# A transformer layer on one core: SP's loads and VectorE's operations in source order, the conditioning row spread by TensorE, exponentials queued behind the last sigmoid

## The chip, the core and the metric

The kernel runs on one core of a Trainium2 chip. Its time is the device time in microseconds of one execution. A core has five engines with a queue each: TensorE (PE in the profile, its weight loads PEld), VectorE (DVE), ScalarE (ACT), GpSimd (POOL) and SyncE (SP), which here only issues DMAs. Each engine does its queue in order, and engines wait for each other by semaphores.

## What is computed

One layer over 1024 latent tokens of 1024 channels, with 256 context tokens. In short:

```python
mod = silu(c) @ w_mod + b_mod                       # six vectors of 1024
h   = x * (1 + scale1) + shift1
h_c = ctx * (1 + scale_c) + shift_c                 # from silu(c_ctx) @ w_mod[:, :2048]
proj = h @ w_in + b_in                              # q_a, k_a, v_a, q_b, k_b, v_b, gate logits
q_a, k_a = rope(...); q_b, k_b = rope(rms_norm(...))
o_a = windowed attention(+-128 tokens, sink) over latent and context keys
o_b = global attention over latent and context keys
y = (sigmoid(g_a) * (o_a @ w_a) + sigmoid(g_b) * (o_b @ w_b)) @ w_out
x = layer_norm(alpha * x + gate1 * y)
x = layer_norm(alpha * x + gate2 * conv_ffn(x * (1 + scale2) + shift2))
```

All is float32. The large products are made of three float32r matmuls: each operand is split into a high part (a cast) and a low part (the difference), and high x high, high x low and low x high are added (`split`, line 79; `mm3`, line 88).

## The kernel before

**First projection (lines 222 to 238).** `h` stands transposed, eight blocks of 128 channels by 1024 tokens. `spread` (line 175) loads c into all 128 partitions by a broadcast DMA and applies Silu, which gives `sc`. For each block k, `load1` fetches two rows of w_mod (`wm`), a block of the weight of q_b (`wr`) and one of x. `modulate` splits the weight (ACT casts the high part, VectorE makes the low part `wlqb`), reduces each `wm` with `sc` on VectorE to a column of `modc` (`mod`, line 186: one multiply-and-add reduction over 128x1024), and makes the high and low parts `hh`, `hl` of h (ACT, ACT, VectorE). Then 24 matmuls add the block to the eight accumulators `q1acc`. `scc`, the same from c_ctx, follows.

**The remaining projections (lines 691 to 738).** `order` is a list of steps: 16 gates (`g`, 48 matmuls each, two halves of 24) are dealt out between the groups qa, qb (8 steps of 12 matmuls each), ka, kb (8 steps of 15: keys and values, four halves of the context among the tiles of kb): 3 gates, qa, 4 gates, qb, 4 gates, ka, 1 gate, kb, 4 gates. `prefetch` (line 616) loads and splits the weights of coming steps; raw weights rotate over 3 buffers and split ones over 8, four pairs. `mods` (line 643) spreads 48 more reductions (`wml` rows of w_mod, 512 KB each) evenly over the steps up to the end of ka: when one is due, it issues its load and its reduction. `gate` ends with a Sigmoid on ACT and a store of the result. `side_step` runs waiting pieces after each step: `qpost` (sums of squares and rotation of queries), `kv_post` (the same for keys, and the splits and transposes `ktr` that fill KL and KC), `qprep` of the first attention units. Accumulators are evacuated at the end of a group by VectorE (`q_evac`; `kv` in line 728).

**What sets the order.** The source gives the dependences; the order on each engine is made by a scheduler with a model of the machine, so an operation can move far from its place in the source. Buffers are reused in rotation: an operation that writes a tile waits for the last use of its buffer. Large temporaries share 19 slots (`ht`, `hput`, lines 129 to 138).

**Passage to the attention (lines 739 to 743).** So that ACT's exponentials, which need another function table than Sigmoid, come behind the last Sigmoid, a tiny chain stands there: VectorE makes zeros out of the last gate's result, ACT takes their Exp, and VectorE adds the zeros to `sinkb`. Then come the attention units (`Unit`, line 383): scores on TensorE, the minimum on VectorE (line 458), Exp on ACT (`soft`, line 424), transposes, values, and the rest of the layer, which the change doesn't touch.

Of the kernel before, what the change touches and what calls it, by code (L numbers as in the profile page):

```python
# [60 lines left out]
VSPAN = 1.0  # L61
VSC = 0, 1
DNS = {u0 + 2 * n + (u0 == 20): (n, j0, j1) for u0, j0, j1 in ((16, 0, 4), (20, 4, 8), (24, 8, 11)) for n in range(3)}


@with_exitstack
def layer_kernel(
# [33 lines left out]
    bmc = ctile([P, 48], F32, "bmc")  # L101
    nc.scalar.dma_start(bmc, bmod)
    modx = ctile([P, 16], F32, "modx")
# [10 lines left out]
    onesf = ctile([P, P], F32, "onesf")  # L114
    mhalf = ctile([P, 8], F32, "mhalf")
    nc.vector.memset(onec, 1.0)
# [89 lines left out]
    def modulate(k):  # L206
        wm, x, wr = st1.pop(k)
        w = wsplit(wr, f"qb{k}")
        for j in (0, 1):
            col = j * 8 + k  # L210
            mod(wm[j], sc, bmc[:, col:col + 1], modc[:, col:col + 1])
        hh = hTp.tile([P, T], R32, tag="hT", name=f"hh{k}", bufs=16)
        hl = hTp.tile([P, T], R32, tag="hT", name=f"hl{k}", bufs=16)
        a, b = modc[:, k:k + 1], modc[:, 8 + k:9 + k]
        for s in [slice(0, HALF), slice(HALF, T)] if k == 0 else [slice(0, T)]:
            nc.scalar.activation(hh[:, s], x[:, s], AF.Identity, bias=a, scale=b)
# [62 lines left out]

    def rms_scale(x3, H, nm, sq, ss=None):  # L280
        nc.scalar.activation(sq.rearrange("p (h d) -> p h d", d=HD), x3, AF.Square)
        if ss is None:
            ss = ph1.tile([P, 8], F32, tag="ss", name=f"ss{nm}", bufs=4)[:, 0:H]
# [21 lines left out]
    def qpost(br, t):  # L305
        q = qtile(br, t)
        q3 = q.rearrange("p (h d) -> p h d", d=HD)
        if br == 0:
            def r0():
                rope(nc.gpsimd if t % 3 == 2 else nc.vector, q, q, 8, ropec[:, t], ropes[:, t], f"q0_{t}")  # L310
            return [r0]
        st = {}

        def s1():
            st["tb"] = ph1.tile([P, 2, HD], F32, tag="tb", name=f"tbq{t}", bufs=4)
            gfold(st["tb"], 0, t, nc.gpsimd)
            rms_scale(q3, 8, f"q{t}", sqq[0][:, t % 2], pqs[:, t])
            if t == NT - 1:
                sqq.clear()
                hput("sqq")  # L320
            nc.gpsimd.tensor_scalar(out=nqs[:, t], in0=pqs[:, t], scalar1=-1.0, scalar2=0.0, op0=ALU.mult, op1=ALU.add)
# [6 lines left out]
    sqq = [ht("sqq", (P, 2, 512))]  # L328
    bias_qb = bias_tile(b_qb, "bias_qb")
    for t in range(NT):  # L330
        q_evac(1, t, acc[t], bias_qb)

    KL, KC, VT = [], [], []
# [7 lines left out]

    def kv_post(t, kv):
        st = {}
        kb = kv[:, 128:256].rearrange("p (h d) -> p h d", d=HD)

        def s1():
            vt = VT[t // 2][:, t % 2]
            v3 = kv[:, 256:512].rearrange("p (h d) -> p h d", d=HD)
# [9 lines left out]

        def s2():
            rms_apply(kb, 2, st["ss"])  # L360
            tp = st["tp"]
# [21 lines left out]
    class Unit:  # L383
# [40 lines left out]
        def soft(self, s, p, h, nm, sm, scale):  # L424
            nc.scalar.activation(p, s, AF.Exp, bias=nm[:, h:h + 1], scale=scale, accum_out=sm[:, h:h + 1])  # L425

# [188 lines left out]

    def prefetch(gi, k):
        if gi == "g":
            hs = []
            for a in (0, 1):
                wr = raw(f"wg{k}_{a}")  # L620
                nc.sync.dma_start(wr.rearrange("p (a b) -> p a b", b=P), w_g[k][:, 4 * a:4 * a + 4])
                hs.append(wsplit(wr, f"g{k}_{a}", "gpsimd"))
            ready[gi, k] = hs
            return
        nm, src, tiles = groups[gi]
        wr = raw(f"w{nm}{k}")
        nc.sync.dma_start(wr, src[k])
        c = None
        if NT in tiles:
            cx = ph1.tile([P, NC], F32, tag="cx", name=f"cx{k}", bufs=2)  # L630
            nc.sync.dma_start(cx, ctxT[k])
            nc.scalar.activation(cx, cx, AF.Identity, bias=modx[:, k:k + 1], scale=modx[:, 8 + k:9 + k])
            c = [ph1.tile([P, NC], R32, tag="ch", name=f"c{a}{k}", bufs=4) for a in "hl"]
            split(cx, *c, nc.vector, nc.vector)
        ready[gi, k] = wsplit(wr, f"{nm}{k}"), c

# [3 lines left out]
    total = len(late)  # L640
    span = [0.0, 0.0]

    def mods(us):
        span[0] += us
        n = total - len(late)
        for _ in range(min(int(total * span[0] / span[1] + 0.01) - n, len(late))):
            col, row, o = late.pop(0)
            w = tmp(f"wml{len(late)}")
            nc.sync.dma_start(w, wmodT[col])
            mod(w, row, bmc[:, col:col + 1], o)  # L650
            if not late:
                hput("sc", "scc")
                kv_alloc()

    def gate(f, hf):
        ps = acc_tile(f"g{f}_{hf}")
        s = slice(hf * HALF, (hf + 1) * HALF)
        for k in range(KT):
            h, l = ready["g", f][k // 4]
            n = slice(k % 4 * P, (k % 4 + 1) * P)  # L660
            mm3(ps, (h[:, n], l[:, n]), (hT[k][0][:, s], hT[k][1][:, s]), k == 0, k == KT - 1)
        if late:
# [4 lines left out]
        nc.scalar.activation(sg, ps, AF.Sigmoid, bias=bgc[:, f:f + 1])  # L667
        nc.scalar.dma_start(sgd[f][:, s], sg)
        return sg

# [25 lines left out]
    ahead = [2 if gi in (0, 2, 3) else 4 for gi, _ in order]  # L696
    span[1] = sum(6 * KT if gi == "g" else 3 * len(groups[gi][2])
                  for gi, _ in order[:order.index((0, KT - 1)) + 1])
    nxt = 0
    for n, (gi, k) in enumerate(order):  # L700
        while nxt < len(order) and sum(ahead[n:nxt + 1]) <= 8:
            prefetch(*order[nxt])
            nxt += 1
        if gi == "g":
            for hf in (0, 1):
                last = gate(k, hf)
                mods(3 * KT)
# [6 lines left out]
        w, c = ready.pop((gi, k))  # L714
        for t in tiles:
            if t < NT:
                s = slice(t * P, (t + 1) * P)
                a = hT[k][0][:, s], hT[k][1][:, s]
            else:
                s = slice((t - NT) * P, (t - NT + 1) * P)  # L720
                a = c[0][:, s], c[1][:, s]
            mm3(acc[t], a, w, k == 0, k == KT - 1)
        mods(3 * len(tiles))
        if k == KT - 1:
            for t in tiles:
                if gi < 2:
                    kv = ph1.tile([P, 512], F32, tag="kv", name=f"kv{t}", bufs=KVB)
                    nc.vector.tensor_tensor(out=kv, in0=acc[t], in1=bias_kv, op=ALU.add)
                    queue.append(kv_post(t, kv))
                else:  # L730
# [11 lines left out]
    nc.scalar.activation(zero, zero, AF.Exp)  # L742
    nc.vector.tensor_tensor(out=sinkb[:, 0:4], in0=sinkb[:, 0:4], in1=zero, op=ALU.add)
    hTp.release()
# [1005 lines left out]
```

## Time and profile before

| | |
|---|---|
| median of 3 runs | 1578.19 us (1576.92 to 1581.11) |
| the profiled execution | 1580.51 us |
| its span in the profile | 1578.6 us, granted clock 0.994 |
| busy PE, DVE, ACT, POOL | 97%, 76%, 51%, 48% of the span |
| first projection q1 starts | 12.87 us |
| first gate starts | 59.06 us |
| attention's first scores | 344.79 us |

The profile is one execution as the hardware profiler took it. A line of a timeline has the start in us, the duration, the engine, the line of the source, the operation, the tile written and those read, the shape, and in brackets how long the engine was idle before and what ended that. A matmul's duration overlaps the next one's; the distance of two starts is the pace. The view of waits has an engine and line, what it waited for, the sum in us, the count and the longest.

### The profile page before, as it was taken

Reading aid. Unit: us, or ns where it says so; the run is one execution under the profiler, and the core shown is the slowest. Engines: PE = TensorE matmul, PEld = TensorE weight load, DVE = VectorE, ACT = ScalarE, POOL = GpSimd, SP = SyncE. Lnnn points to the kernel's source line nnn. Section 1 sums busy time; section 2 is a strip of 40 time slices with the busy share of each in tenths; the row PEclk is TensorE's granted clock in tenths of the full one; section 3 lists DMA queues with packets and bytes.
Section 4 is the critical chain, followed back from the end, with each engine's and each line's share of the span. In section 5 each row is a group of like instructions: output and inputs, shape, how many; then the busy total and the mean of one; then the engine's idle time right before and its main releaser. Section 6 shows DMA issues by size and latency. Waiting matters only on the chain.

```text
span 1578.6 us, 21930 instructions
## 1 busy us (share of the span) xinstructions
PE 1528.4 (97%) x7614; PEld 1264.6 (80%) x7614; DVE 1198.0 (76%) x1761; ACT 808.9 (51%) x1439; POOL 756.5 (48%) x737
## 2 busy tenths in 40 slices
PE   6999999999999999999999999999999999999997
PEld 5878788878886887777788898888888888888886
DVE  7797645628888777788675679888888888656797
ACT  5422222448888667688522466444444444435533
POOL 0573312426666566655432544666667765021053
PEclk9999999999999999999999999999999999999999
DMA  9685662322227555532344132333334446996723
GB/s 378 218 313 187 213 219 87 120 79 74 64 82 180 138 128 127 128 84 41 130 160 93 54 107 81 121 107 107 107 107 107 107 111 178 364 270 221 244 92 107
DMA packets 112015, 230.25 MB, mean 146 GB/s; under 512 B 13504, under 2 KB 27328, under 8 KB 111808
## 3 DMA queue, kind: packets, MB, share of 16 engines
q1 hardware_dynamic: 96464, 199.20, 37.9%
q0 software_dynamic: 10400, 20.19, 8.2%
q10 hardware_dynamic: 5040, 9.46, 1.6%
q8 instruction: 60, 0.98, 0.3%
q14 instruction: 51, 0.42, 0.1%
HBM read 177.61 MB, written 65.87 MB: 154 GB/s over the span
## 4 chain that ended last, share of the span: by engine, by line
PE 73%; DVE 12%; DMA 5%; ACT 4%; issue 3%; POOL 1%; SPq 0%; ACTq 0%; DVEq 0%; POOLq 0%
PE ptr L530 5%; PE b L91 3%; PE b L90 3%; PE b L89 3%; PE g L89 3%; PE g L91 3%; PE g L90 3%; PE s L413 2%; PE av L551 2%; PE c L90 2%; PE d L90 2%; PE a L90 2%; PE c L89 2%; PE d L89 2%; PE a L89 2%
## 5 line engine op out<-in xcount | busy, mean ns | idle before, releaser
L540 DVE TENSOR_TENSOR ptl<-ptr,pth 128x512 fp32r<-128x512 f32 x188 | 124.6, 684 | 27.8 <-ACT pth L539 25.6
L86 DVE TENSOR_TENSOR ld<-rd,hd 128x1024 fp32r<-128x1024 f32 x77 | 97.6, 1284 | 50.8 <-ACT hd L81 48.7
L530 PE MATMUL ptr<-ident,p 128*128 128x128 f32 x816 | 126.7, 278 | 9.2 <-DVE ptl L540 6.8
L539 ACT CAST pth<-ptr 128x512 fp32r<-128x512 f32 x188 | 106.5, 588 | 56.5 <-PE ptr L530 32.8
L425 ACT ACTIVATE p<-p,nm 128x1024 f32<-128x1024 f32 (+2 forms) x128 | 125.3, 981 | 11.1 <-DVE p L458 10.3
L530 PEld LDWEIGHTS ptr<-ident,p 128*128 128x128 f32 x816 | 93.6, 140 | 39.6 <-DVE ptl L540 13.9
L81 ACT CAST hd<-rd 128x1024 fp32r<-128x1024 f32 x77 | 79.4, 1050 | 88.5 <-PE p L91 60.4
L551 PE MATMUL av<-pth,VT 128*128 128x512 f32 x236 | 104.6, 443 | 1.0 <-ACT avs L557 0.5
L90 PE MATMUL p<-ld,hd 128*128 128x512 f32 x264 | 103.5, 392 | 0.3 <-DVE ld L86 0.3
L89 PE MATMUL p<-hd 128*128 128x512 f32 x264 | 103.8, 393 | 0.0
L91 PE MATMUL p<-hd,ld 128*128 128x512 f32 x264 | 103.5, 392 | 0.0
L89 PE MATMUL g<-hh,whg 128*128 128x512 f32 x256 | 99.9, 390 | 0.0
L91 PE MATMUL g<-hh,wlg 128*128 128x512 f32 x256 | 99.7, 389 | 0.0
L90 PE MATMUL g<-hl,whg 128*128 128x512 f32 x256 | 99.6, 389 | 0.0
L552 PE MATMUL av<-ptl,VT 128*128 128x512 f32 x236 | 97.7, 414 | 1.9 <-POOL ptl L86 1.8
L86 POOL TENSOR_TENSOR wlg<-wg,whg 128x512 fp32r<-128x512 f32 x32 | 44.2, 1388 | 112.7 <-ACT whg L81 109.2
L458 DVE TENSOR_SCALAR_CACHE_REDUCE p<-s,cvt,nmc 128x1024 f32<-128x1024 f32 x64 | 84.4, 1339 | 12.3 <-PE s L414 11.8
L413 PE MATMUL s<-KL,q 128*128 128x512 f32 (+2 forms) x192 | 76.0, 396 | 2.9 <-ACT p_x L425 2.0
L187 DVE CUSTOM_DVE_ANT_0 wml<-wml,sc,bmc 128x1024 f32<-128x1024 f32 x32 | 45.6, 1435 | 40.6 <-DMA wml<-in_wmodT_dram 39.7
L83 POOL TENSOR_SCALAR pth<-prw 128x512 fp32r<-128x512 f32 x48 | 31.0, 646 | 87.8 <-ACT prw L536 62.3
L414 PE MATMUL s<-KL,q 128*128 128x512 f32 (+2 forms) x192 | 71.7, 373 | 0.0
L81 ACT CAST wS<-s 128x512 fp32r<-128x512 f32 x76 | 45.3, 621 | 51.0 <-POOL s L1083 50.2
(402 smaller groups left out, 4945.7 us busy)
## 6 DMA issues: line engine op xcount, KB each, us to landing
wml<-in_wmodT_dram SPq DMA_DIRECT2D x48, 512.0 KB
ru<-in_w_up_dram SPq DMA_DIRECT2D x38, 512.0 KB
rd<-td SPq DMA_DIRECT2D x55, 256.0 KB
rd<-sd SPq DMA_DIRECT2D x44, 256.0 KB
rd<-in_w_dn_dram SPq DMA_DIRECT2D x33, 256.0 KB
wm<-in_wmodT_dram SPq DMA_DIRECT2D x16, 512.0 KB
wg<-in_w_g_dram SPq DMA_DIRECT2D x32, 256.0 KB
sgd<-sg ACTq DMA_DIRECT2D x32, 256.0 KB
```

Of the source, the lines that this page charges most:

```text
L81: cast[:] = [nc.scalar.copy(hi, src).ins]
L86: low[:] = [lo_eng.tensor_tensor(out=lo, in0=src, in1=hi.bitcast(F32), op=ALU.subtract).ins]
L89: nc.tensor.matmul(ps, a[0], b[0], start=start, stop=False, skip_group_check=resumed)
L90: nc.tensor.matmul(ps, a[0], b[1], start=False, stop=False, skip_group_check=resumed)
L91: nc.tensor.matmul(ps, a[1], b[0], start=False, stop=stop, skip_group_check=resumed)
L413: nc.tensor.matmul(o, self.q[0][:, hs], ks, start=True, stop=False)
L425: nc.scalar.activation(p, s, AF.Exp, bias=nm[:, h:h + 1], scale=scale, accum_out=sm[:, h:h + 1])
L530: nc.tensor.transpose(tr[:, h * P:(h + 1) * P], self.pslice(h, n), ident)
L539: nc.scalar.copy(hi, tr)
L540: nc.vector.tensor_tensor(out=lo, in0=tr, in1=hi.bitcast(F32), op=ALU.subtract)
L551: nc.tensor.matmul(self.av, v, hi, start=first, stop=False)
L552: nc.tensor.matmul(self.av, v, lo, start=False, stop=self.left == 0)
```

## The change

- c is loaded as one row of 4 KB. TensorE spreads it over the partitions: two float32 matmuls with a row of ones; Silu reads the halves from PSUM. Five matmuls of ones by ones stand ahead of them and twelve behind, whose results nobody uses. In block 0 the weight's split comes behind the two reductions.
- The sums of squares of q_b are made for two tiles at a time, ahead of their rotation: four instructions of double width on ACT, VectorE and GpSimd in place of eight.
- `prefetch` is taken apart: loads (`wload1`) run 5 steps ahead of the matmuls, splits (`wpair`) 3; a gate counts as two steps. The loads of `wml` (`mload`) run 4 ahead of the reductions. From there to the end of ka, SP and VectorE keep the source's order (`manual_schedule`); the other engines, and the rest of the kernel, are left to the scheduler.
- The evacuation of keys and values moves from the group's end into the first piece of `kv_post`.
- The chain of zeros goes. One Exp of 8 columns with nothing to compute is issued behind the last Sigmoid, and each `soft` behind it.

```diff
+WARM = 5, 12
+WLOAD = 5
+WSPLIT = 3
+MLOAD = 4
...
-    nc.scalar.dma_start(bmc, bmod)
...
+    crow = hp.tile([1, D], F32, tag="H18", name="crow", bufs=1)
+    nc.scalar.dma_start(crow, c_row.rearrange("(a d) -> a d", a=1))
+    nc.scalar.dma_start(bmc, bmod)
...
     def modulate(k):
         wm, x, wr = st1.pop(k)
-        w = wsplit(wr, f"qb{k}")
+        if k:
+            w = wsplit(wr, f"qb{k}")
         for j in (0, 1):
             col = j * 8 + k
             mod(wm[j], sc, bmc[:, col:col + 1], modc[:, col:col + 1])
+        if k == 0:
+            w = wsplit(wr, f"qb{k}")
...
-    spread(sc, c_row, 0)
+    cb = [acc_tile(f"cb{n}") for n in (0, 1)]
+    for n in range(WARM[0]):
+        nc.tensor.matmul(cb[1][:, 0:P], onesf, onesf, start=True, stop=True)
+    for n in (0, 1):
+        s = slice(n * HALF, (n + 1) * HALF)
+        nc.tensor.matmul(cb[n], onesf[0:1], crow[:, s], start=True, stop=True)
+        nc.scalar.activation(sc[:, s], cb[n], AF.Silu)
+    wt_ = acc_tile("warm")
+    for n in range(WARM[1]):
+        nc.tensor.matmul(wt_[:, 0:P], onesf, onesf, start=True, stop=True)
...
         def s1():
             st["tb"] = ph1.tile([P, 2, HD], F32, tag="tb", name=f"tbq{t}", bufs=4)
             gfold(st["tb"], 0, t, nc.gpsimd)
-            rms_scale(q3, 8, f"q{t}", sqq[0][:, t % 2], pqs[:, t])
...
+            if t % 2 == 0:
+                qstats(t)
...
+    def qsquare(t):
+        nc.scalar.activation(sqq[t // 2 % 2].rearrange("p a b -> p (a b)"), Q[1, t].rearrange("p a b -> p (a b)"),
+                             AF.Square)
+
+    def qstats(t):
+        sq = sqq[t // 2 % 2]
+        ss, ns = (a[:, t:t + 2].rearrange("p a b -> p (a b)") for a in (pqs, nqs))
+        nc.vector.tensor_reduce(out=ss, in_=sq.rearrange("p a (h d) -> p (a h) d", d=HD), axis=AX.X, op=ALU.add)
+        if t + 4 < NT:
+            qsquare(t + 4)
+        nc.vector.tensor_scalar(out=ss, in0=ss, scalar1=1.0 / HD, scalar2=QK_EPS, op0=ALU.mult, op1=ALU.add)
+        nc.gpsimd.tensor_tensor(out=ss, in0=ss, in1=mhalf[:, 0:16], op=ALU.pow)
+        nc.gpsimd.tensor_scalar(out=ns, in0=ss, scalar1=-1.0, scalar2=0.0, op0=ALU.mult, op1=ALU.add)
...
         def s1():
+            kv = st["kv"] = ph1.tile([P, 512], F32, tag="kv", name=f"kv{t}", bufs=KVB)
+            nc.vector.tensor_tensor(out=kv, in0=acc, in1=bias_kv, op=ALU.add)
...
         def soft(self, s, p, h, nm, sm, scale):
-            nc.scalar.activation(p, s, AF.Exp, bias=nm[:, h:h + 1], scale=scale, accum_out=sm[:, h:h + 1])
+            with tc.issue_after(first_exp):
+                nc.scalar.activation(p, s, AF.Exp, bias=nm[:, h:h + 1], scale=scale, accum_out=sm[:, h:h + 1])
...
+    def mload():
+        col, row, o = late.pop(0)
+        w = tmp(f"wml{len(late)}")
+        nc.sync.dma_start(w, wmodT[col])
+        coming.append((col, row, o, w))
...
-            col, row, o = late.pop(0)
-            w = tmp(f"wml{len(late)}")
-            nc.sync.dma_start(w, wmodT[col])
+            col, row, o, w = coming.pop(0)
             mod(w, row, bmc[:, col:col + 1], o)
-            if not late:
+            if late:
+                mload()
+            elif not coming:
...
+    held = steps.index((0, KT - 1, 0)) + 1
+    inorder = ExitStack()
+    inorder.enter_context(tc.manual_schedule(engines={mybir.EngineType.DVE, mybir.EngineType.SP}))
+    for n in range(WLOAD):
+        at(n, wload1)
+        if n + WSPLIT - WLOAD >= 0:
+            at(n + WSPLIT - WLOAD, wpair)
+    for _ in range(MLOAD):
+        mload()
+    for n, (gi, k, a) in enumerate(steps):
+        if n == held:
+            inorder.close()
+        at(n + WLOAD, wload1)
+        at(n + WSPLIT, wpair)
+        at(n + 3, cload, 1)
+        at(n + 2, cpair, 1)
...
-    zero = ph1.tile([P, 4], F32, tag="zero", name="zero")
-    nc.vector.tensor_scalar(out=zero, in0=last[:, 0:4], scalar1=-(2.0 ** 100), scalar2=None, op0=ALU.min)
-    nc.scalar.activation(zero, zero, AF.Exp)
-    nc.vector.tensor_tensor(out=sinkb[:, 0:4], in0=sinkb[:, 0:4], in1=zero, op=ALU.add)
+    with tc.issue_after(sigmoid[0]):
+        first_exp = nc.scalar.activation(lnx[:, 0:8], negsink, AF.Exp).ins
```

More of the change, by code (lines that the diff above doesn't have):

```diff
@@ L114, in layer_kernel @@
     onesf = ctile([P, P], F32, "onesf")
[L115 removed]
+    mhalf = ctile([P, 24], F32, "mhalf")
     nc.vector.memset(onec, 1.0)
@@ L278, in gfold, with rms_scale @@
             eng.tensor_tensor(out=dv[:, :, a, :], in0=sv[:, :, a, :], in1=gv[:, :, 1 - a, :], op=ALU.mult)
-    def rms_scale(x3, H, nm, sq, ss=None):
+    def rms_scale(x3, H, nm, sq):
         nc.scalar.activation(sq.rearrange("p (h d) -> p h d", d=HD), x3, AF.Square)
-        if ss is None:
-            ss = ph1.tile([P, 8], F32, tag="ss", name=f"ss{nm}", bufs=4)[:, 0:H]
+        ss = ph1.tile([P, 8], F32, tag="ss", name=f"ss{nm}", bufs=4)[:, 0:H]
         nc.vector.tensor_reduce(out=ss, in_=sq.rearrange("p (h d) -> p h d", d=HD), axis=AX.X, op=ALU.add)
@@ L326, in qpost @@
         return [s1] + [lambda: None] * GAP + [s2]
-    sqq = [ht("sqq", (P, 2, 512))]
+    sqq = [ht(f"sqq{n}", (P, 2, 512)) for n in (0, 1)]
+    def qsquare(t):
[10 more added lines that the diff above has]
+        nc.gpsimd.tensor_scalar(out=ns, in0=ss, scalar1=-1.0, scalar2=0.0, op0=ALU.mult, op1=ALU.add)
+        if t + 2 == NT:
+            hput("sqq0", "sqq1")
     bias_qb = bias_tile(b_qb, "bias_qb")
@@ L331, in layer_kernel @@
         q_evac(1, t, acc[t], bias_qb)
+        if t in (1, 3):
+            qsquare(t - 1)
     KL, KC, VT = [], [], []
@@ L340, in layer_kernel, with kv_post @@
     bias_kv = bias_tile(b_kv, "bias_kv")
-    def kv_post(t, kv):
+    def kv_post(t, acc):
         st = {}
-        kb = kv[:, 128:256].rearrange("p (h d) -> p h d", d=HD)
         def s1():
+            kv = st["kv"] = ph1.tile([P, 512], F32, tag="kv", name=f"kv{t}", bufs=KVB)
+            nc.vector.tensor_tensor(out=kv, in0=acc, in1=bias_kv, op=ALU.add)
+            kb = st["kb"] = kv[:, 128:256].rearrange("p (h d) -> p h d", d=HD)
             vt = VT[t // 2][:, t % 2]
@@ L359, in s2 @@
         def s2():
+            kv, kb = st["kv"], st["kb"]
             rms_apply(kb, 2, st["ss"])
@@ L614, in layer_kernel, with wload1, wpair, cload @@
     ready = {}
-    def prefetch(gi, k):
+    def wload1(gi, k, a):
         if gi == "g":
[L618 to L635, printed above, removed]
+            wr = raw(f"wg{k}_{a}")
+            nc.sync.dma_start(wr.rearrange("p (a b) -> p a b", b=P), w_g[k][:, 4 * a:4 * a + 4])
+        else:
+            wr = raw(f"w{groups[gi][0]}{k}")
+            nc.sync.dma_start(wr, groups[gi][1][k])
+        ready[gi, k, a, "raw"] = wr
+    def wpair(gi, k, a):
+        wr = ready.pop((gi, k, a, "raw"))
+        if gi == "g":
+            ready[gi, k, a] = wsplit(wr, f"g{k}_{a}", "gpsimd")
+        else:
+            ready[gi, k, a] = wsplit(wr, f"{groups[gi][0]}{k}")
+    def cload(gi, k):
+        cx = ready["cx", k] = ph1.tile([P, NC], F32, tag="cx", name=f"cx{k}", bufs=2)
+        nc.sync.dma_start(cx, ctxT[k])
+    def cpair(gi, k):
+        cx = ready.pop(("cx", k))
+        nc.scalar.activation(cx, cx, AF.Identity, bias=modx[:, k:k + 1], scale=modx[:, 8 + k:9 + k])
+        c = ready["c", k] = [ph1.tile([P, NC], R32, tag="ch", name=f"c{a}{k}", bufs=4) for a in "hl"]
+        split(cx, *c, nc.vector, nc.vector)
     late = [(col, scc, modx[:, col:col + 1]) for col in range(16)]
@@ L641, in layer_kernel @@
     span = [0.0, 0.0]
+    coming = []
+    def mload():
[3 more added lines that the diff above has]
+        coming.append((col, row, o, w))
     def mods(us):
         span[0] += us
-        n = total - len(late)
-        for _ in range(min(int(total * span[0] / span[1] + 0.01) - n, len(late))):
-            col, row, o = late.pop(0)
-            w = tmp(f"wml{len(late)}")
-            nc.sync.dma_start(w, wmodT[col])
+        n = total - len(late) - len(coming)
+        for _ in range(min(int(total * span[0] / span[1] + 0.01) - n, total - n)):
+            col, row, o, w = coming.pop(0)
             mod(w, row, bmc[:, col:col + 1], o)
-            if not late:
+            if late:
+                mload()
+            elif not coming:
                 hput("sc", "scc")
                 kv_alloc()
+    sigmoid = []
     def gate(f, hf):
@@ L658, in gate @@
         for k in range(KT):
-            h, l = ready["g", f][k // 4]
+            h, l = ready["g", f, k // 4]
             n = slice(k % 4 * P, (k % 4 + 1) * P)
             mm3(ps, (h[:, n], l[:, n]), (hT[k][0][:, s], hT[k][1][:, s]), k == 0, k == KT - 1)
-        if late:
+        if late or coming:
             sg = ht(f"sg{f}_{hf}", (P, HALF))
@@ L695, in layer_kernel, with at @@
             order += [(gi, k) for k in range(KT)]
-    ahead = [2 if gi in (0, 2, 3) else 4 for gi, _ in order]
     span[1] = sum(6 * KT if gi == "g" else 3 * len(groups[gi][2])
                   for gi, _ in order[:order.index((0, KT - 1)) + 1])
[L699 to L703, printed above, removed]
+    steps = [(gi, k, a) for gi, k in order for a in ((0, 1) if gi == "g" else (0,))]
+    def at(n, fn, *only):
+        if n < len(steps) and (not only or steps[n][0] in only):
+            gi, k, a = steps[n]
+            fn(*((gi, k) if only else (gi, k, a)))
+    held = steps.index((0, KT - 1, 0)) + 1
[14 more added lines that the diff above has]
+        at(n + 2, cpair, 1)
         if gi == "g":
-            for hf in (0, 1):
-                last = gate(k, hf)
-                mods(3 * KT)
+            gate(k, a)
+            mods(3 * KT)
+            side_step()
+            if not (late or coming):
                 side_step()
@@ L713, in layer_kernel @@
             slow[0] = gi > 1
-        w, c = ready.pop((gi, k))
+        w = ready.pop((gi, k, 0))
+        c = ready.pop(("c", k), None)
         for t in tiles:
@@ L726, in layer_kernel @@
                 if gi < 2:
-                    kv = ph1.tile([P, 512], F32, tag="kv", name=f"kv{t}", bufs=KVB)
-                    nc.vector.tensor_tensor(out=kv, in0=acc[t], in1=bias_kv, op=ALU.add)
-                    queue.append(kv_post(t, kv))
+                    queue.append(kv_post(t, acc[t]))
                 else:
```

13 lines of the change are left out of this document (4 added, 9 removed).

## The prediction

> **What bounds the kernel now.** The page's first line gives the span that all sums below use; the kernel ran 1580.51 us in that profiled execution, 1.9 us more than its span, against a median of 1578.19 us (1576.92 to 1581.11).
>
> ```profile
> span 1578.6 us, 21930 instructions
> ```
>
> Next the windows view in stretches of 10 us over the first 440 us: after the stretch come its length, then the busy time of PE, PEld, DVE, ACT and POOL, each with a count, then PEclk, DMA share and GB/s. Nearly every stretch has PE busy for all of its 10 us. Among those that don't, before the attention starts:
>
> ```profile
> 90.00:100.00 10.00, 7.80 (x34) 5.89 (x32) 9.87 (x16) 2.86 (x5) 8.79 (x6) 1.00 0.87 297
> 100.00:110.00 10.00, 9.31 (x35) 7.59 (x36) 10.00 (x19) 1.24 (x2) 5.87 (x6) 0.83 0.90 320
> 170.00:180.00 10.00, 7.86 (x33) 5.58 (x32) 6.35 (x11) 1.86 (x3) 0.00 (x0) 1.00 0.75 252
> ```
>
> TensorE bounds this phase, and what can be won is its holes. The waits of PE up to 420 us name who ends them:
>
> ```profile
> PE q1acc L89 <- ACT hh L216: 12.9, 1, 12.9
> PE accqb L90 <- DVE wlqb L86: 2.6, 3, 1.5
> PE accqa L90 <- DVE wlqa L86: 2.4, 1, 2.4
> PE str L497 <- DVE sm L493: 1.2, 1, 1.2
> PE s L413 <- ACT KC L380: 0.6, 1, 0.6
> ```
>
> So there are four places: the start, a wait for a weight's low part in the projection accqa, three in accqb, and the passage to the attention (str, s).
>
> The start, in the timeline (start, duration, engine, instruction, idle time before it):
>
> ```profile
> 0.86 0.17 DVE L117 MEMSET onesf<- 128x128 f32 x1
> 4.75 0.17 DVE L224 TENSOR_SCALAR bmc<-bmc 128x8 f32<-128x8 f32 x1 [3.70 <-DMA bmc<-in_bmod_dram]
> 7.77 1.06 ACT L179 ACTIVATE sc<-row 128x1024 f32<-128x1024 f32 x1 [4.83 <-DMA row<-in_c_row_dram]
> 10.07 0.69 DVE L86 TENSOR_TENSOR wlqb<-wr,whqb 128x512 fp32r<-128x512 f32 x1
> 10.67 1.28 DVE L187 CUSTOM_DVE_ANT_0 wm<-wm,sc,bmc 128x1024 f32<-128x1024 f32 x1
> 12.00 1.52 ACT L216 ACTIVATE hh<-xr,modc 128x512 fp32r<-128x512 f32 x2 [2.66 <-DVE modc L187]
> 12.87 0.79 PE L89 MATMUL q1acc<-whqb,hh 128*128 128x512 f32 x1 [12.87 <-ACT hh L216]
> 59.06 0.39 PE L89 MATMUL g<-hh,whg 128*128 128x512 f32 x1
> ```
>
> The broadcast load of c ends at 7.77, Silu at 8.83, and the two reductions into modc stand with the split wlqb between them. From 12.87 to 59.06 run the 192 matmuls of q1.
>
> The other holes, in PE's timeline:
>
> ```profile
> 97.78 0.50 PE L89 MATMUL accqa<-whqa,hh 128*128 128x512 f32 x1 [0.48 <-ACT whqa L81]
> 100.69 0.80 PE L90 MATMUL accqa<-wlqa,hh 128*128 128x512 f32 x1 [2.41 <-DVE wlqa L86]
> 101.29 0.63 PE L91 MATMUL accqa<-whqa,hl 128*128 128x512 f32 x1
> 103.72 0.40 PE L91 MATMUL accqa<-whqa,hl 128*128 128x512 f32 x1
> 118.27 0.39 PE L89 MATMUL g<-hh,whg 128*128 128x512 f32 x1
> 167.22 0.39 PE L89 MATMUL accqb<-whqb,hh 128*128 128x512 f32 x1
> 178.81 0.50 PE L90 MATMUL accqb<-wlqb,hh 128*128 128x512 f32 x1 [1.51 <-DVE wlqb L86]
> 183.06 0.40 PE L90 MATMUL accqb<-wlqb,hh 128*128 128x512 f32 x1
> ```
>
> The pace: 64 steps from 103.72 to 118.27, 0.227 us each. By it q1's 192 steps need 43.6 us and took 46.2: 2.6 us lost to half clock and first waits. From 97.78 to 103.72 stand 8 steps, 1.8 us of work in 5.9; with the 0.48 before them and the slow restart 4.7 us are lost. From 167.22 to 183.06 stand 52 steps, 11.8 us of work in 15.8: 4.0 lost.
>
> Why the splits were late: the scheduler had filled SP's queue with modulation rows (wml) that waited for free slots, the weight loads stood behind them, and VectorE did what had come.
>
> ```profile
> 89.41 9.92 SPq L649 DMA_DIRECT2D wml<-in_wmodT_dram  x5
> 97.83 2.26 POOL L270 TENSOR_TENSOR Q<-rt1q,rt2q 128x512 f32<-128x512 f32 x1
> 98.90 1.74 DVE L86 TENSOR_TENSOR wlqa<-wqa,whqa 128x512 fp32r<-128x512 f32 x1
> ```
>
> **The change part by part. The start.** A row of 4 KB replaces 512 KB. Two float32 matmuls spread it and Silu works by halves. The row's landing is not in the trace; the nearest rows bound it: 1.23 us for a small row to DRAM, and 4.0 us for bmc (issued at 0.72, awaited until 4.75).
>
> ```profile
> 419.29 1.23 DMA dn<-rb
> 877.80 1.02 PE L1047 MATMUL bcra<-dgra,onesf 128*128 128x512 f32 x2
> 878.66 1.02 PE L1047 MATMUL bcma<-dgma,onesf 128*128 128x512 f32 x2
> ```
>
> A float32 matmul of 512 columns takes 0.86 us at full clock, 1.7 at half; one of 128 columns a quarter, 0.43 at half. The five warming ones run from 1.03 (onesf) to 3.2, so a row that lands before 3.2 costs nothing; bmc's end would be 4.75. I take 3.5, nearer to bmc with its many rows, but ahead of it in its queue. Then at half clock the spreads end at 5.2 and 6.9, the second half of Silu (0.6 to 0.7, as for other 128x512 activations) at 7.55 instead of 8.83. The two reductions now follow each other (1.2 apiece), without the 0.60 of wlqb between: hh starts at about 10.1 and PE 0.87 later at 10.95: 1.9 us earlier. By 4.75 Silu ends at 8.8 and only the 0.6 is left. The twelve matmuls behind the spreads need 2.6 us at full clock, 5.2 at half, from 6.9: done between 9.5 and 12.1. They wait for nothing and end before hh unless the clock stays low.
>
> The clock: in this trace PE came to full pace at 103.72, 3.0 us after its restart at 100.69, and the idle 1.51 us before 178.81 did not slow it. With work from 1.0 on, q1 should begin at full clock, and the 2.6 us go. The Trainium skill, "TensorE: Matmul & The Clock Gate", section "What's actually happening", says that the activity window is free-running, of some 3.4 us; so the wait for the row could spoil one window, and by that rule part of the 2.6 would come back in some executions. The 3.0 us above agrees with it. Against that, the operands of the second of the eight contraction blocks come hardly faster: its hh waits on ACT for Silu of the context's row.
>
> ```profile
> 15.89 1.06 ACT L179 ACTIVATE scc<-row 128x1024 f32<-128x1024 f32 x1 [0.45 <-DMA row<-in_cc_row_dram]
> ```
>
> With 512 KB less ahead of it that may come at 14.5; PE would be through block 0 at 16.7, and Silu and hh need 1.06 + 1.5 us after it: I book 0.8 us of new waits (0 to 1.5). Start in all: -1.9 - 2.6 + 0.8 = -3.7.
>
> **SP and VectorE in source order.** No operation is added. Five weight loads and four wml run ahead, a split is three steps ahead of its matmuls, and each wml is loaded four reductions before its use: 48 rows over 840 matmuls, one per 17.5, so four of them are 15.9 us. The longest landing of a wml in the chain of waits is 5.2, so what is queued behind a reduction on VectorE no longer waits for DMA. Does VectorE keep up? A split waits until PE has left the step four before, since four pairs of buffers rotate. From there to the last qa step PE has 3 half gates (24 matmuls each) and 7 steps of 12: 156 x 0.227 = 35.4 us. In the built order VectorE has in that stretch 8 splits, 6 reductions, 3 rotations and 2 sums of squares:
>
> ```profile
> 167.04 5.17 DMA wml<-in_wmodT_dram
> L187 DVE CUSTOM_DVE_ANT_0 wml<-wml,scc,bmc x16: 1271/1274/2298, 59.9 to 112.2; 128x1024 f32<-128x1024 f32 x16
> ```
>
> With 0.69 a split, 1.28 a reduction (the median), three passes of 0.7 a rotation and 1.5 for two tiles' squares (twice a 128x512 pass) that is 5.5 + 7.7 + 6.3 + 3.0 = 22.5 us of 35.4. The slack is 13 us; behind the split that waits for the first qa step, 3 splits, 2 reductions, a rotation and a pair of squares, 8.2 us, stand against the 16.3 of six steps. So I count both groups of holes as gone: -4.7 and -4.0. The reduction's maximum of 2.298 gives the other bound: if all that VectorE does there were stretched by 2.298/1.28, 22.5 would be 40 us, 5 us too long. The Trainium skill, "SBUF — State Buffer", section "Who interferes with whom", calls the port pair that VectorE and GpSimd share an exclusive lock, the loser blocked for the whole instruction; the row at 98.90, one split of 1.74 us beside GpSimd's 97.83 where the other splits take 0.69, agrees. By that rule an order in which VectorE can't step aside loses those 5 us in accqa, which is rival (b). The merged sums of squares take instructions off VectorE and GpSimd beside PE's work; I cost them at nothing, hidden by the same slack.
>
> **Keys.** The evacuations kv move into the first step of kv_post, and the transposes ktr stand one or two steps earlier in PE's order, so the first waits on ks.
>
> ```profile
> 256.18 1.28 DVE L728 TENSOR_TENSOR kv<-accka,bias_kv 128x512 f32<-128x512 f32 x2
> 262.81 0.42 DVE L86 TENSOR_TENSOR ks<-kv,ks 128x256 fp32r<-128x256 f32 x1
> ```
>
> That was 6.6 us after accka ended at 256.2; PE now has two half gates (10.9 us) before it, but the fourth and fifth transposes come with hardly any slack. I book +0.7 (0 to 3).
>
> **Passage to the attention.**
>
> ```profile
> 344.26 0.39 PE L91 MATMUL g<-hh,wlg 128*128 128x512 f32 x1
> 345.87 1.28 ACT L742 ACT_TABLE_LOAD   x1
> 348.27 0.72 ACT L425 ACTIVATE p<-p,nm 128x512 f32<-128x512 f32 x1 [0.90 <-DVE p L458]
> ```
>
> Now the last context transpose and its copy KC stand before the last gates, so the 0.6 us wait goes, and no VectorE instruction waits for the table's load. The first exponential comes 4.0 us after the last gate's last matmul. The new order puts the copy of q before it, which needs PE's four scores and transpose: 3.8. But the following exponentials are no longer split by that copy: each comes 0.7 earlier. I take -0.7 (0 to -2).
>
> Sum: -3.7 - 4.7 - 4.0 + 0.7 - 0.7 = -12.4 us, against 1580.5 in the profiled run 1568.1; on the median 1565.8. Behind the passage PE's order is nearly unchanged, so the lead should reach the end.
>
> **Rivals.** (a) The start gains nothing but the 0.6: the row lands like bmc and the clock is still low. For it: bmc's 4.0 us. Then -0.6 - 4.7 - 4.0 + 0.0 = -9.3: 1568.9. (b) The holes only shrink: VectorE was busy 10.00 of 10 us in 100 to 110, and slowed by GpSimd as the longest reductions were it keeps half of the two holes (4.4 us) while ktr costs its 3. Then -3.7 - 4.4 + 3 - 0.7 = -5.8: 1572.4. (c) Slower: strict order stops the queue's head. A weight load on SP waits for a raw buffer that a split on VectorE frees, the split stands behind a reduction, and its wml stands behind that load. It decides when SP falls more than 15.9 - 5.2 = 10.7 us behind. Then each reduction shows its 5.2: six in accqa make 22.5 + 31 = 54 of 35.4, 18 us lost, as much in accqb, with the start's gain 1578.2 - 3.7 + 36 = 1610. Against it: the raw buffers are free about when PE leaves an earlier step. (d) The change does less than it says: the lead runs out later, since other queues set the end of the attention: 1577.
>
> **How the numbers follow.** The forecast 0.60, (a) 0.13, (b) 0.15, (c) 0.07, (d) 0.05. The likeliest is 1565.8, and its own bounds are -16 to -9. The range 1562 to 1573 takes in (a) and (b) and leaves out (c), (d) and the ends of the unknown costs. 0.3% (4.7 us) is about what a measurement of this kernel can tell from no change. Faster by more: 0.60 + 0.13 + 0.12 of (b) = 0.85; within 0.08; slower 0.07.
>
> **What would show it.** In the changed kernel's timeline: q1's first matmul near 10.95 at a pace of 0.227, the first g near 55.3; no wait of PE for wlqa or wlqb; no long idle of VectorE for wml; the last gate some 12 us earlier than 344.26. A q1 start after 12, a pace of 0.43 there, PE waiting for ks, or an SP row as long as 9.92 before a weight load would show where it is wrong.

## The result, and the profile after

The changed kernel takes 1581.11 us (median of 20 runs, 1577.74 to 1584.61) against 1578.44 us before (20 runs, 1575.45 to 1581.11): ratio 1.0017, 95% interval 1.0011 to 1.0023. The forecast was 1565.8 us. So 15 us of the forecast gain are missing, and the question is where they went.

The profiled execution of the changed kernel ran 1577.74 us, its fastest of the 20; that of before, 1580.51 us, lies near the top of its 20. The two spans stand 2.6 us the wrong way round for that reason, and the comparison below goes by stages.

The first line of the page, the windows, and the waits of PE up to 420 us (lines left out are marked), in the same views as for the kernel before:

```profile
span 1576.0 us, 21965 instructions
```

```profile
90.00:100.00 10.00, 10.00 (x46) 8.29 (x45) 9.88 (x17) 2.80 (x5) 8.31 (x9) 1.00 0.51 153
100.00:110.00 10.00, 10.00 (x46) 8.29 (x45) 9.90 (x14) 2.49 (x4) 8.74 (x8) 1.00 0.72 246
110.00:120.00 10.00, 10.00 (x46) 8.28 (x45) 10.00 (x15) 1.94 (x3) 6.87 (x6) 1.00 0.52 160
170.00:180.00 10.00, 10.00 (x46) 8.28 (x45) 6.92 (x9) 1.87 (x3) 6.00 (x4) 1.00 0.76 255
```

```profile
PE ptr L567 <- ACT p L462: 1.4, 1, 1.4
PE cb L233 <- DVE mhalf L121: 1.1, 1, 1.1
...
PE g L95 <- POOL wlg L90: 0.4, 1, 0.4
```

PE is now busy all of the 10 us where it had 7.80, 9.31 and 7.86, and no wait for wlqa or wlqb is left. The rows that the prediction named, in the timeline of the changed kernel:

```profile
1.08 2.50 PE L233 MATMUL cb<-onesf 128*128 128x128 f32 x10 [1.08 <-DVE mhalf L121]
3.51 3.78 PE L236 MATMUL cb<-crow,onesf 1*128 1x512 f32 x4
7.22 4.82 PE L240 MATMUL warm<-onesf 128*128 128x128 f32 x24
10.50 1.52 ACT L225 ACTIVATE hh<-xr,modc 128x512 fp32r<-128x512 f32 x2 [2.06 <-DVE modc L193]
11.79 0.48 PE L93 MATMUL q1acc<-whqb,hh 128*128 128x512 f32 x1
55.43 0.47 PE L93 MATMUL g<-hh,whg 128*128 128x512 f32 x1
56.77 0.50 PE L95 MATMUL g<-hh,wlg 128*128 128x512 f32 x1 [0.40 <-POOL wlg L90]
110.62 0.39 PE L93 MATMUL g<-hh,whg 128*128 128x512 f32 x1
171.37 0.39 PE L94 MATMUL accqb<-wlqb,hh 128*128 128x512 f32 x1
332.52 0.40 PE L95 MATMUL g<-hh,wlg 128*128 128x512 f32 x1
336.07 0.72 ACT L462 ACTIVATE p<-p,nm 128x512 f32<-128x512 f32 x1
```

The first gate comes 3.63 us earlier than before (where it stood at 59.06), the gate behind qa 7.65 (118.27), the step of qb behind its last hole 11.69 (183.06), the last gate's last matmul 11.74 (344.26), the first exponential 12.20 (348.27). The forecast had 12.4 us there. So nearly all that was forecast had arrived at 336 us, and it was lost later.

Most of where it went is seen in two instructions that both kernels have far behind: the first matmul of the stage `a`, and the first of `yl`. Between them PE has the same matmuls in the same order. First the kernel before, then the changed one:

```profile
985.83 0.39 PE L89 MATMUL a<-B,wA 128*128 128x512 f32 x1
1533.37 0.28 PE L89 MATMUL yl<-hd 128*128 128x256 f32 x1
```

```profile
972.87 0.40 PE L93 MATMUL a<-B,wA 128*128 128x512 f32 x1
1530.94 0.28 PE L93 MATMUL yl<-hd 128*128 128x256 f32 x1
```

The lead is still 12.96 us at `a`, and 2.43 us at `yl`. The same stretch took 547.54 us before and 558.07 after, 1.9% more. It isn't a wait. In the windows view, first of before (three rows), then of after, PE is busy for 20 of 20 us at a granted clock of 1.00 in both from 1400 us on; but where 90 matmuls went in 20 us, 88 go. The two other rows of before, with a clock of 0.91, are moments of reduced clock; they are taken up below.

```profile
780.00:800.00 20.00, 18.20 (x73) 14.31 (x72) 13.29 (x12) 5.87 (x6) 2.69 (x4) 0.91 0.51 179
1400.00:1420.00 20.00, 20.00 (x90) 16.57 (x89) 11.36 (x12) 7.92 (x8) 5.15 (x6) 1.00 1.04 268
1500.00:1520.00 20.00, 19.46 (x85) 15.65 (x84) 18.15 (x22) 9.35 (x11) 8.56 (x5) 0.91 0.55 179
```

```profile
1400.00:1420.00 20.00, 20.00 (x88) 16.09 (x87) 11.37 (x12) 7.34 (x7) 4.30 (x5) 1.00 1.06 282
```

And the groups of PE from 1340 to 1500 us (count, busy time, mean ns of one), first before (one of three, all with 389 ns), then after, show that each matmul is longer, 394 to 397 ns where it was 389:

```profile
L89 PE MATMUL p<-hd 128*128 128x512 f32 x225 | 87.5, 389 | 0.0
```

```profile
L93 PE MATMUL p<-hd 128*128 128x512 f32 x225 | 89.4, 397 | 0.0
L94 PE MATMUL p<-ld,hd 128*128 128x512 f32 x225 | 88.9, 395 | 0.0
L95 PE MATMUL p<-hd,ld 128*128 128x512 f32 x225 | 88.6, 394 | 0.0
```

Nothing of the change's schedule reaches these stages. One line of the full diff does. It is not among the lines shown with the change above, which have only its use, `mhalf[:, 0:16]`, and the prediction has no term for it:

```diff
-    mhalf = ctile([P, 8], F32, "mhalf")
+    mhalf = ctile([P, 24], F32, "mhalf")
```

This constant holds -0.5 and is the last in the first of the pools that are filled from the left end of SBUF; other pools are filled from the right end. With 16 more columns of 4 bytes, every tile behind it on the left lies 64 bytes higher in each partition. In the built programs, from the attention on, the operands of the large products on both sides began at 224 bytes past a multiple of 256; now those on the left begin at 32, and a matmul can have one operand of each kind. (A trace doesn't show these places.) The matmuls of the gates have both operands on the right, and keep their pace. So the rest of the layer, whose source the change doesn't touch, is touched through its addresses.

### The profile page after: what moved, and what is told of

The parts are those of the page before. It is cut to its first block, busy times and chain, and to the rows that moved or that the text cites. A ratio compares the mean times of both kernels' runs of the same rounds, so it can differ in the third digit from the quotient of the medians.

```text
span 1576.0 us, 21965 instructions
## 1 busy us (share of the span) xinstructions
PE 1544.8 (98%) x7652; PEld 1267.3 (80%) x7652; DVE 1190.3 (76%) x1751; ACT 810.1 (51%) x1436; POOL 759.5 (48%) x729
## 4 chain that ended last, share of the span: by engine, by line
PE 85%; DVE 8%; ACT 4%; issue 2%; POOL 1%; DMA 0%; DVEq 0%; SPq 0%; ACTq 0%; POOLq 0%
PE ptr L567 5%; PE g L95 4%; PE p L93 4%; PE g L94 4%; PE g L93 4%; PE p L94 4%; PE p L95 4%; PE b L95 3%; PE b L94 3%; PE b L93 3%; PE s L449 2%; PE av L588 2%; PE c L93 2%; PE d L94 2%; PE a L95 2%; PE s L450 2%
## 5 line engine op out<-in xcount | busy, mean ns | idle before, releaser
L495 DVE TENSOR_SCALAR_CACHE_REDUCE p<-s,cvt,nmc 128x1024 f32<-128x1024 f32 x64 | 84.4, 1339 | 12.6 <-PE s L450 12.4
L85 ACT CAST wA<-ru 128x512 fp32r<-128x512 f32 x57 | 35.4, 621 | 66.7 <-PE d L95 36.3
```

Source lines behind the costliest of these rows:

```text
L85: cast[:] = [nc.scalar.copy(hi, src).ins]
```

## The experiments

Two theories stood against each other. **Theory A:** the pace of a matmul depends on where its operands begin in SBUF. **Theory R:** the pace is a state of TensorE, or comes from other engines' traffic. One fact speaks for a state: in the kernel before, the granted clock fell to 0.91 in the window from 780 to 800 us, ahead of the fast stretch, and in the changed kernel it did not.

**Moving the left tiles.** Four kernels change only the width of mhalf.

```diff
 e1_m40, e3_m32, e4_m16 (changed kernel), e2_b24 (kernel before)
-    mhalf = ctile([P, 24], F32, "mhalf")
+    mhalf = ctile([P, 40], F32, "mhalf")      # e1; e3: 32; e4: 16
-    mhalf = ctile([P, 8], F32, "mhalf")
+    mhalf = ctile([P, 24], F32, "mhalf")      # e2
```

> The changed kernel with the constant mhalf 40 columns wide instead of 24 (nothing reads the new columns): every tile that lies on the left of SBUF moves up by 64 bytes, so left and right tiles all start at 96 mod 128, as from the attention on in the kernel before. Theory A, the changed kernel's matmuls run at 0.232 us instead of 0.227 from the attention on because mhalf grew from 8 to 24 columns and put the left tiles at 32 mod 128: pace 0.227 to the end, the lead of 13.5 us at 950 us is kept, 1565 to 1568 us, 0.992 of the kernel before. Theory R, the pace is a state of TensorE that the half-clock window at 790 us in the kernel before had reset, or traffic of other engines: addresses don't matter, 1581 us, ratio 1.002.

> The kernel before with the constant mhalf 24 columns wide instead of 8 and nothing else: left tiles at 32 mod 128. Theory A: its first 340 us as before, then the pace 0.231 to 0.234 in the streams of matmuls after the attention; the changed kernel lost 13.5 us between 790 and 1500 us so, hence 1590 to 1594 us, ratio 1.008. Theory R: 1578 us, ratio 1.000.

> The changed kernel with mhalf 32 columns wide: left tiles at 64, right tiles at 96 mod 128. Theory A in the form A1 (moving data and weights must start at the same place in 128 bytes): mixed, so slow as in the changed kernel, 1578 to 1582 us. In the form A2 (only a start at 32 is slow): 1565 to 1568 us. Theory R: 1581 us at 0.232.

> The changed kernel with mhalf 16 columns wide, which is all that the change reads: left tiles at 0, right tiles at 96 mod 128. A1: slow, 1578 to 1582 us. A2: 1565 to 1568 us. Theory R: 1581 us.

| kernel | left tiles mod 256 | us | ratio to before (interval) |
|---|---|---|---|
| e2_b24 | 32 | 1594.16 | 1.0097 (1.0078 to 1.0116) |
| e1_m40 | 96 | 1579.54 | 1.0004 (0.9993 to 1.0015) |
| e3_m32 | 64 | 1581.71 | 1.0017 (1.0006 to 1.0027) |
| e4_m16 | 0 | 1581.64 | 1.0019 (1.0008 to 1.0030) |

The places are those of the left tiles of the large products; right ones stay at 224. e2_b24 decides for A: 64 bytes in the kernel before, and nothing else, cost 15.7 us (1594.16 - 1578.46), just past the 1590 to 1594 that A had given, where R had 1578. Its stretch from `a` to `yl` takes 558.08 us, as in the changed kernel, and `p<-hd` has the same 397 ns:

```profile
989.84 0.40 PE L89 MATMUL a<-B,wA 128*128 128x512 f32 x1
1547.92 0.28 PE L89 MATMUL yl<-hd 128*128 128x256 f32 x1
```

```profile
L89 PE MATMUL p<-hd 128*128 128x512 f32 x201 | 79.8, 397 | 0.0
```

But e1_m40, for which A had forecast 1565 to 1568, was a miss: left tiles begin at 96 and right ones at 224 there, which agree mod 128, and it is slow all the same. e3_m32 and e4_m16 lie in the 1578 to 1582 of form A1 and rule out A2, by which only a start at 32 is slow. Thus the theory was mended: left and right have to agree mod 256 (A3).

Moments of reduced clock do not go with the pace either. In e1_m40 the clock fell to 0.95 in the window from 780 to 800 us and to 0.91 from 860 to 880, and its `p` matmuls still take 392 to 396 ns; e7_cold (below) has 1.00 in every window of 20 us from 20 to 1540 us, and takes 389 to 390 ns.

**Back to 224 mod 256.** The next width that does it on the changed kernel, 72 columns, is more than SBUF holds. So mhalf goes back to 8 columns, and the one operation that needs 16 is made twice.

```diff
-    mhalf = ctile([P, 24], F32, "mhalf")
+    mhalf = ctile([P, 8], F32, "mhalf")
...
-        nc.gpsimd.tensor_tensor(out=ss, in0=ss, in1=mhalf[:, 0:16], op=ALU.pow)
+        for h in (0, 8):
+            nc.gpsimd.tensor_tensor(out=ss[:, h:h + 8], in0=ss[:, h:h + 8], in1=mhalf, op=ALU.pow)
```

> The changed kernel with mhalf 8 columns wide as before the change; the power of -0.5 over 16 columns is two operations of GpSimd over 8 (four small operations more in all). Left tiles start at 224 mod 256 again, as the right ones do from the attention on. Theory A3 (what counts is the start mod 256: left and right must agree there; 96 in place of 224 was not enough): pace 0.227 after the attention, the lead of 13.5 us is kept, 1564 to 1568 us, ratio 0.991 to 0.993. Theory R (not addresses but a state of TensorE or other engines' traffic, which an earlier end of the first phase brings on): 1579 to 1582 us, pace 0.231.

Measured: 1567.05 us against 1577.67, ratio 0.9925 (0.9912 to 0.9937). The stretch takes 547.24 us again, and the matmul 389 ns:

```profile
974.66 0.39 PE L93 MATMUL a<-B,wA 128*128 128x512 f32 x1
1521.90 0.28 PE L93 MATMUL yl<-hd 128*128 128x256 f32 x1
```

```profile
L93 PE MATMUL p<-hd 128*128 128x512 f32 x234 | 91.0, 389 | 0.0
```

Not all of the difference stands in the two rows above. The stretch of e5_m8 has one window at 0.91 (1500 to 1520 us), as that of before has. The two kernels with equal places and no such window in it, e7_cold and e9_w12 below, need 545.40 us (971.89 to 1517.29) and 545.53 (972.94 to 1518.47). So the unequal places cost about 12.6 us in this stretch. Ahead of it, the stretch from the first matmul of `u` to `a` takes 70.2 to 70.3 us in all five kernels with unequal places and 69.5 in all four with equal ones. Where the rest of some 15 us goes is not shown.

The two effects multiply: 0.9925 for the schedule times 1.0097 for the 64 bytes (e2_b24) is 1.0021, and the change as it came measured 1.0017 (1.0011 to 1.0023).

**Matmuls alone.** Is it TensorE by itself, or does it need the other engines? The next kernel leaves the layer out and does nothing but matmuls. The first line below names two of its 16 blocks.

```python
# BLOCKS has ("wb", ((0, 32),)), ("ma", ((0, 0), (64, 64))), ...
for nm, offs in BLOCKS:
    for g in range(4):
        ps = psp.tile([P, 512], F32, tag="acc", name=f"{nm}{g}")
        for n in range(24):
            m, w = offs[n % len(offs)]
            nc.tensor.matmul(ps, wt(n % 8, w // 4), mv(n % 6, m // 4), start=n == 0, stop=n == 23)
```

> Only matmuls (fp32r, 128x512, a new weight for each), in 16 blocks of 96 from one tile that starts at 0 mod 256; nothing of the layer is computed, and the output is a copy of the last sums. In a block moving data and weight start at m and w bytes past a multiple of 256: same 0/0, wa 0/16, wb 0/32, wc 0/64, wd 0/96, we 0/128, wf 0/192, wg 0/224, wh 0/256, ba 32/32, bb 64/64, bc 224/224; ma alternates 0/0 and 64/64, mb 0/0 and 128/128, mc takes 0/0, 0/64, 64/0 in turn; back 0/0. Theory A3: same, wh, ba, bb, bc, back take 0.2267 us a matmul, 21.8 us a block; wb to wg and ma, mb, mc 0.231 to 0.234, 22.2 to 22.4 a block, with no other engine at work. Theory R: all blocks 21.8 us.

The groups of PE, one for each block of 96 matmuls (busy us, mean ns; 8 of the 16):

```profile
L120 PE MATMUL wc<-buf 128*128 128x512 f32 x96 | 22.6, 396 | 0.0
L120 PE MATMUL wb<-buf 128*128 128x512 f32 x96 | 22.6, 395 | 0.0
L120 PE MATMUL ma<-buf 128*128 128x512 f32 x96 | 22.4, 394 | 0.0
L120 PE MATMUL wf<-buf 128*128 128x512 f32 x96 | 22.1, 391 | 0.0
L120 PE MATMUL mb<-buf 128*128 128x512 f32 x96 | 22.1, 390 | 0.0
L120 PE MATMUL back<-buf 128*128 128x512 f32 x96 | 21.9, 389 | 0.0
L120 PE MATMUL wh<-buf 128*128 128x512 f32 x96 | 21.9, 389 | 0.0
L120 PE MATMUL wa<-buf 128*128 128x512 f32 x96 | 21.9, 389 | 0.0
```

A block's busy time less its last matmul, over 95 steps, is the pace: (21.9 - 0.389)/95 = 0.226 us with equal places (back, and 0/256 in wh), (22.6 - 0.396)/95 = 0.234 us at 32 or 64 bytes apart (wb and wc), some 3% more. At 96 bytes apart (wd) a matmul has 396 ns as well, at 224 (wg) 395, at 128 (we) 394. The first block, same, has 416 ns because it holds the slow steps of the start; back repeats it. From 20 to 360 us no other engine was at work, so R falls in its second form too. At which place a kernel's tiles begin doesn't matter as long as they agree (ba, bb and bc, at 32, 64 and 224, took 389 ns a matmul). In ma each matmul's own pair agrees and only the neighbours differ, and it is slow. It was not foreseen that 0/192 (wf) and the alternation by 128 (mb) would cost less than half as much. For the 16 bytes of wa nothing had been forecast; it goes at full pace.

> Matmuls alone again, blocks of 96 (nothing of the layer is computed); moving data and weight at m/w bytes past a multiple of 256. Question: which pair has to agree, a matmul's own moving data and weight, or its moving data and the weight that is loaded beside it for the next matmul. own alternates 0/64 and 64/0 (own pair differs, moving and next weight agree), next alternates 0/0 and 64/64 (own agree, next differ); ownb and nextb the same with 160. If the load beside it counts: own and ownb 0.2267 us a matmul, next and nextb 0.231 to 0.234. If the own pair counts: the other way round. If all neighbours must agree: all four slow. wh 0/8, wi 0/24, wj 0/28: 0.2267 if 32 bytes are one place; wk 16/32: slow if places are cut at multiples of 32, fast if only a distance under 32 counts; wl 0/240 and mw 64/0 slow. three takes the changed kernel's places in stage p: 32/32, 224/32, 32/224: about 0.233. back 0.2267.

```profile
L119 PE MATMUL own<-buf 128*128 128x512 f32 x96 | 22.6, 396 | 0.0
L119 PE MATMUL wk<-buf 128*128 128x512 f32 x96 | 22.6, 396 | 0.0
L119 PE MATMUL three<-buf 128*128 128x512 f32 x96 | 22.5, 395 | 0.0
L119 PE MATMUL next<-buf 128*128 128x512 f32 x96 | 22.4, 394 | 0.0
L119 PE MATMUL back<-buf 128*128 128x512 f32 x96 | 21.9, 389 | 0.0
```

This kernel, too, leaves the layer out. Both own and next are slow (as are ownb, 392 ns, and nextb, 396): neither pair alone explains it, all neighbours must agree. `three` repeats the changed kernel's places in stage `p`, and gives 395 ns, as there. Even 8 bytes apart (the wh of this kernel, 0/8) cost 4 ns, 24 (wi) 4 and 28 (wj) 5, so the idea that 32 bytes are one place is wrong; wl (0/240) costs 1 and mw (64/0) 3. 16 apart isn't free in itself (wk, 16/32, costs 7), which leaves wa's 0/16 unexplained. So the rule in use is "equal mod 256": equal places were never slow here, and it is not shown which unequal ones are free. What it is in the chip that collides stays open.

**The warming matmuls.** Two kernels on top of e5_m8 test the prediction's start.

```diff
-WARM = 5, 12
+WARM = 0, 0       # e7_cold
+WARM = 0, 12      # e9_w12
```

> The kernel of e5_m8 without the 17 warming matmuls (those over ones, whose sums nobody reads); the two that spread c stay. If they bring the full clock at q1, its first matmuls run at 0.43 us a step again until about 16 us and 1.5 to 3 us of the lead go: 1.5 to 3 us more than e5_m8. If the two spreading matmuls and the free-running clock window do it without them: the same as e5_m8 within 0.5 us.

> The kernel of e5_m8 without the five warming matmuls ahead of the spread, with the twelve behind it. If the five only stand in the way of the row (it has landed by 2.7 us, the spread began at 3.5): spread at 2.7, q1's first matmul at 10.6 to 10.9 instead of 11.63, at full clock: a lead of 0.8 us more in the first phase, 1566 us. If they are what brings the full clock early: q1 begins at 0.43 us a step and the lead is that of e7_cold, 0.65 us less than e5_m8. Either way the time is within 1 us of e5_m8, about what a few rounds can't tell; the trace decides.

e7_cold: 1566.68 us, ratio 0.9927 (0.9912 to 0.9943). e9_w12: 1567.65 us, 0.9942 (0.9922 to 0.9963). Neither can be told from e5_m8 by its time, so the 1.5 to 3 us that e7_cold should have lost are not seen. The timelines of PE, e7_cold and then e9_w12, tell more:

```profile
10.49 0.80 PE L93 MATMUL q1acc<-whqb,hh 128*128 128x512 f32 x1 [4.07 <-ACT hh L225]
11.09 0.63 PE L94 MATMUL q1acc<-wlqb,hh 128*128 128x512 f32 x1
15.82 0.40 PE L93 MATMUL q1acc<-whqb,hh 128*128 128x512 f32 x1
```

```profile
2.27 3.75 PE L236 MATMUL cb<-crow,onesf 1*128 1x512 f32 x4 [2.27 <-DMA crow<-in_c_row_dram]
5.95 5.49 PE L240 MATMUL warm<-onesf 128*128 128x128 f32 x24
11.09 0.72 PE L93 MATMUL q1acc<-whqb,hh 128*128 128x512 f32 x1
11.65 0.39 PE L94 MATMUL q1acc<-wlqb,hh 128*128 128x512 f32 x1
```

Without any warming q1 begins at 10.49 at half pace and has it until 15.8; with the twelve behind the spread it begins at 11.09 and is at full pace from its second matmul on. So the twelve bring the clock, at the price of keeping q1 waiting. What that is worth is small: the first matmul of accqa starts at 89.35 us in e7_cold and at 88.70 in e5_m8, 0.65 us apart. The five ahead only delay the spread, to 3.51 us from 2.27 (e9_w12) or 2.68 (e7_cold), when the row has landed; without them accqa starts at 88.44, 0.26 us earlier, where 0.8 had been expected. (The clock of the start is read from the pace here: the windows view of e7_cold gives 1.00 from 12 to 16 us too, where the steps are 0.43 us.)

## Why the prediction was wrong

**The step that failed** is the last of the working: "Behind the passage PE's order is nearly unchanged, so the lead should reach the end." The order is unchanged (from `a` to `yl` the two built programs have the same matmuls, one for one), but the operands lie elsewhere. The working went through the moved instructions and never through the memory that the change allots; the wider `mhalf` stood in the full diff and got no cost. It costs some 15 us (15.7 in e2_b24), more than the whole gain.

**The start** (forecast -3.7): -3.63 at the first gate, with terms that were off against each other. q1 began at 11.79, not 10.95. The spread began at 3.51, where 3.5 had been taken, but that was luck: 3.5 stood for the landing of the row, and what the spread waited for was the five warming matmuls. hh was under way from 10.50, not 10.1, and the twelve others, mostly at half clock, ran from 7.22 to 12.04, the upper end of what was worked out, and held q1 back (0.87 us behind the start of hh, as before, would be 11.37). In exchange q1's 192 steps took 43.64 us (11.79 to 55.43), 0.227 each: the half clock went entirely from q1, and none of the 0.8 us booked for new waits in q1 came. Behind it, at 56.77, came a wait of 0.40 us for the first wlg that wasn't foreseen; with what stood around it 0.8 us went there (accqa starts 2.84 us earlier, at 88.86 instead of 91.70). Rival (a) is wrong on both counts: the row has landed by 2.3 to 2.7 us (e9_w12, e7_cold), not at 4.75, and q1 has its full pace.

The clock came to full pace at most 4.6 us after 7.22 here, 5.3 us after 10.49 in e7_cold. Counted from 1.08, where PE's first matmuls start, it would be up to 10.7 us; the five and the two spreads, of one row each, kept PE nearly busy until 7.2 and did not bring the clock. Why they didn't is not shown. The Trainium skill, "TensorE: Matmul & The Clock Gate", section "What's actually happening", has a free-running window of about 3.4 us that must be busy. By an estimate from that figure, a start within a window costs between one and two of them, 3.4 to 6.8 us; the 4.6 and 5.3 agree with it, the 10.7 does not.

**The holes** (-4.7 and -4.0): the lead grew from 2.84 to 7.65 us by 110.62 and to 11.69 by 171.37, that is -4.8 and -4.0. Rival (b) expected VectorE to fall behind. It came nearer to that than the 13 us of slack suggest. In the stretch that the working counted, here 72.50 to 107.90 us, VectorE was busy 26.65 of 35.40 us and not 22.5, a slack of 8.7: it did eight reductions and four rotations where six and three had been counted. From 90 to 120 us it was busy 9.88 to 10.00 of every 10 us, and some operations beside GpSimd's work were stretched, as in this row of the changed kernel, a reduction of 2.31 us instead of 1.28:

```profile
109.38 2.31 DVE L193 CUSTOM_DVE_ANT_0 wml<-wml,scc,bmc 128x1024 f32<-128x1024 f32 x1
```

That PE never waited there is put down to the three steps that the splits run ahead; no run varies them. Rival (c) did not occur: of waits for a weight only the 0.40 us for wlg is left.

**Keys** (+0.7): 0.0; from 171.37 to the last gate the lead stays, 11.69 and 11.74. **Passage** (-0.7): -0.46, from 11.74 to 12.20.

**Rival (d)**, "the lead runs out later", has the right shape and nearly the time (1577), but not the cause: no other queue sets the end. PE's waits behind 420 us are nearly those of before. The largest was 6.7 us then, and is now:

```profile
PE ptr L567 <- DVE ptl L577: 6.0, 11, 1.6
```

With the tiles where they were, the sum was right: 0.9925 of 1578.4 is 1566.6 us (1564.5 to 1568.5 by the interval), and 1565.8 was forecast. Part of that is luck: the +0.7 for keys that didn't come and the 0.8 lost at the first wlg stand against each other.

## What to carry to other kernels

A diff changes memory as well as work: work out which pools move, and by how many bytes, before the gain of a schedule is carried to the end. Where PE is busy all the time and still slower, compare the count of matmuls in a window and the mean of one group, not the waits. For streams of fp32r matmuls like these keep the tiles of moving data and of weights at the same place mod 256 bytes, and after a new constant pad the pool or find its bytes elsewhere.

## What the runs showed of the hardware that was not expected

A 128x512 fp32r matmul with a new weight takes 0.226 us a step when all operands begin at the same place mod 256 bytes, and up to 0.234 when they don't (e6_pace), at a granted clock of 1.00 in every window of 20 us from 20 to 360 us and with no wait in the trace. The Trainium skill, "SBUF — State Buffer", section "Operand start alignment", asks only that an operand begin at a multiple of its element size, and says of its measurements that they timed nothing. For these matmuls e2_b24 puts a price on the place, 15.7 us of 1578 for 64 bytes.

Moments of reduced clock in the middle of a run (0.91 in the windows of 20 us from 780 and from 1500 us of the profiled kernel before, none from 20 to 1560 us in the changed one) differ between executions: the mean granted clock of the kernel before goes from 0.993 to 0.999 over its executions. By an estimate from the two rows (0.09 of 20 us, twice) they cost the profile of before 3.6 us. That is part of why the two profiled executions, 1580.51 and 1577.74 us, look as if the change had won 2.8 us where the medians show 2.7 us lost.
